# Attention of a hybrid trunk: probabilities turned in 32x32 blocks on VectorE, and every engine in a written order

## The chip, the cores and the metric

The kernel runs on one core of one Trainium2 chip. The metric is the device time of one launch in microseconds (us), the lower the better. A comparison of two kernels takes several runs of each on the same chip. Times of single instructions and waits come from one profiled execution of a kernel.

The engines are named as the profile names them: PE is TensorE (matmuls), PEld its weight loads, DVE is VectorE, ACT is ScalarE, POOL is GpSimd, and SP is the engine from whose queue most loads are issued. Each has its own instruction stream and runs it in order; semaphores connect them. Data lies in SBUF, with 128 partitions, and in PSUM, into which PE writes, here in banks of 512 fp32 columns.

## What is computed

Two layers over 512 latent tokens and 128 context tokens of width 1024. Layer 0 is grouped-query attention with 16 query heads over 4 key/value heads of 64 dimensions; layer 1 is a gated linear recurrence. Both have an adaLN modulation and a post-LayerNorm. The change is in layer 0. The part of the reference that it touches:

```python
def _block_attention(q, k, v):
    ...
    def one_block(q_blk):
        s = jnp.einsum('bqkgd,bskd->bkgqs', q_blk.astype(jnp.float32), kf) * scale
        p = jax.nn.softmax(s, axis=-1)
        return jnp.einsum('bkgqs,bskd->bqkgd', p, vf).astype(q.dtype)

def _attn_latent(h, ctx_k, ctx_v, w_in, q_gain, k_gain, w_out):
    q, k, v, g = _attn_project(h, w_in, q_gain, k_gain)
    ...
    keys = jnp.concatenate([ctx_k.astype(k.dtype), k], axis=1)
    vals = jnp.concatenate([ctx_v.astype(v.dtype), v], axis=1)
    o = _block_attention(q, keys, vals)
    return _attn_out(o, g, w_out)
```

`_attn_project` has the RMS norm of queries and keys, the lines left out the rotary positions, and `_attn_out` multiplies by silu(g) and by `w_out`. Latent queries read 640 keys, 128 cached and 512 latent; context queries read the 128 context keys. All is fp32. Projections and scores split an operand into a high and a low part (type fp32r) and add the products; the product of probabilities and values is a plain fp32 matmul, which stands as two matmul instructions in the trace.

## The kernel before

The program has a lead-in (modulation, key/value projection, first query projection, gate projections), a woven attention, the output projection with the norm, and the recurrent layer. The change is in the woven attention, which goes over the 4 key/value heads `c`, each with 4 query heads `h`.

*A front* (`front`, L812) is one query head and 128 latent queries: four matmuls, two halves of 320 keys by a high and a low key part (`score_mms`, L722), into one of two double banks. DVE takes the negated maximum (L817), ACT the exponential with its sum (L820). Two calls later (`defer`, L733, and `tick`, L739), DVE takes the reciprocal and POOL scales the probabilities `p` (L824, L825). There are 64 fronts and four of the prompt (`prompt_unit`, L767).

*The turn* (`trans`, L828): the product with the values needs keys on partitions, so PE transposes `p` into PSUM, in ten 128x128 pieces per unit of two fronts (L832), and ACT or DVE copies them to SBUF (`keep_pt`, L726).

*The product* (`apply`, L841): for two heads and 256 queries, five key blocks of 128; the values are the stationary operand (128 keys by 64 columns, `vv`, L499), and the two heads lie in the two halves of the array's columns (`av_mms`, L747). DVE multiplies the result into the gate `gs` in place (L755).

Between these run side jobs: the query projections of heads 1 to 3 (`q_gen`, L591: 15 token tiles of 24 matmuls, norm and rotary positions on DVE, a split and transposes), 16 chunks of the modulation (`ada_gen`, L308, whose weights stream in from DRAM), the split of the gated result (`split_gs`, L941) and two pieces of the output weights. `att_gen` (L851) and `weave` (L85) make the source order: 0.7 steps of the side jobs after each step of attention. The engines don't follow that order strictly: a scheduler of the tile layer places each engine's instructions by priority and estimated readiness, so that one that is ready can go ahead of one that waits. SP's loads go through a queue of their own in the order of `order` (L366), two pieces ahead (`pump`, L196).

Of the kernel before, what the change touches and what calls it, by code (L numbers as in the profile page):

```python
# [11 lines left out]
F32 = mybir.dt.float32  # L12
# [21 lines left out]
ADA_CUT = (4, 8, 12)  # L34
# [6 lines left out]
D_SCALE = 2  # L41
D_OUTS = 2
SIDE_T = 2.2
SIDE_B = 0.7
# [87 lines left out]
def hybrid_step(ctx: ExitStack, tc: tile.TileContext, a: dict, o: dict):  # L132
# [141 lines left out]
    def ada_row(ps):  # L274
        row = rowp.tile([P, CW], F32, tag="row", name="row")
        nc.vector.tensor_copy(row, ps[:, :CW])
        return row
# [30 lines left out]
    def ada_gen(chunks):  # L308
        todo, last = None, None
        for l, c in chunks:  # L310
            ps = bank1("adaps")
            ada_mms(ps, l, c, 0)
            if last:
                last()
            last = todo and ada_out(*todo)
            yield
            ada_mms(ps, l, c, 1)
            yield
            todo = (l, c, ada_row(ps))
        if last:  # L320
            last()
        if todo:
            last = ada_out(*todo)
            yield
            if last:
                last()
                yield

# [30 lines left out]
    ADA_AT = (0,) + ADA_CUT + (len(ADA),)  # L359
    ADA_B = [ADA[ADA_AT[n]:ADA_AT[n + 1]] for n in range(4)]  # L360

# [6 lines left out]
    for c in range(3):  # L368
        order.extend(pieces("attn_w_in", c + 1))
        order.extend(ada_pieces(ADA_B[c]))  # L370
    order.extend(ada_pieces(ADA_B[3]))
    order.extend(("attn_w_out", nh, i) for nh, i in PIECES)
# [53 lines left out]
    with pool("xin", 1) as xin:  # L426
        rope = xin.tile([P, 2, TS, HD], F32, name="rope")
        ck = prep.tile([P, CW], F32, tag="ck", name="ck")
# [44 lines left out]
        for ft in range(KT):  # L473
# [4 lines left out]
            row = ada_row(ps)  # L478
# [20 lines left out]
    vv = kvp.tile([P, 6, CW], F32, name="vv")  # L499
# [18 lines left out]
    def rms_apply(ps, n, rstd, off=0):  # L518
        w = n * CW
        qn = prep.tile([P, 2 * CW], F32, tag="qn", name="qn")  # L520
# [5 lines left out]
    def rope_apply(qn, tt0, n, cos, sin, g, r=None):  # L526
# [3 lines left out]
        if tt0 == TS:  # L530
# [3 lines left out]
        u = prep.tile([P, 2 * CW], F32, tag="u", name="u")  # L534
        nc.vector.tensor_tensor(heads4(u[:, :w], n), heads4(qn[:, :w], n),
                                view(sin, tt0 * HD, [[HD, n], [0, 4], [1, HD]]), ALU.mult)
        nc.vector.tensor_tensor(heads4(r[:, :w], n), heads4(qn[:, :w], n),
                                view(cos, tt0 * HD, [[HD, n], [0, 4], [1, HD]]), ALU.mult)
# [29 lines left out]
    def q_split(r, tt0, n, odd, X, alloc):  # L568
# [4 lines left out]
        nc.vector.tensor_tensor(view(s2, HD * (1 - odd), [[P, 4 * n], [1, HD]]), rv, hv.bitcast(F32), ALU.subtract)  # L573
# [11 lines left out]
    def tok_unit(w, tt0, n, name):  # L585
        ps = bank1(name)
        for i in range(n):
            yield from tok_gen(ps[:, i * CW:(i + 1) * CW], w, tt0 + i, hhi, hlo)
        return ps

    def q_gen(c, X):  # L591
        w = Weights("attn_w_in", c, (nc.vector, nc.vector))
        yield
        yield
        pend = None
        for tt0, n in UNITS:
            ps = yield from tok_unit(w, tt0, n, "qmm")
            rstd = rms_stat(ps, n)
            yield
            if pend:  # L600
                for i in range(pend[1]):
                    pend[0](i)
                    yield
            else:
                yield
            yield
            qn = rms_apply(ps, n, rstd)
            r = rope_apply(qn, tt0, n, cosq, sinq, qg)
            yield
            pend = (q_split(r, tt0, n, c % 2, X, bank1), n)  # L610
        yield
        for i in range(pend[1]):
            pend[0](i)
            yield
# [124 lines left out]
    def tick():  # L739
# [4 lines left out]
        for _, fn in due:  # L744
            fn()
# [757 lines left out]
```

## Time and profile before

| | |
|---|---|
| median of three runs | 892.8 us (889.97 to 896.09) |
| the profiled execution | 891.1 us, of which the span of instructions is 889.3 |
| busy share of the span | PE 95%, DVE 61%, ACT 42%, POOL 24% |
| woven attention | 138.8 to 368.0 us |
| lead-in before it, from the gate projections on | 75.0 to 138.8 us |
| output projection, norm and recurrent layer after it | 368.0 to 889 us |

A row of a group reads: line, engine, operation, output<-inputs, shape, count | busy us, mean ns of one | idle time of the engine just before them and what ended it. Tile shapes of matmuls such as 128\*64 are rows by columns of the array. A row of waits reads: who waited <- for what: us in total, times, longest. Matmuls are pipelined, so that their durations overlap; the distance of two starts is what one costs in a stream.

### The profile page before, as it was taken

Reading aid. Unit: us, or ns where it says so; the run is one execution under the profiler, and the core shown is the slowest. Engines: PE = TensorE matmul, PEld = TensorE weight load, DVE = VectorE, ACT = ScalarE, POOL = GpSimd, SP = SyncE. Lnnn points to the kernel's source line nnn. Section 1 sums busy time; section 2 is a strip of 40 time slices with the busy share of each in tenths; the row PEclk is TensorE's granted clock in tenths of the full one; section 3 lists DMA queues with packets and bytes.
Section 4 is the critical chain, followed back from the end, with each engine's and each line's share of the span. In section 5 each row is a group of like instructions: output and inputs, shape, how many; then the busy total and the mean of one; then the engine's idle time right before and its main releaser. Section 6 shows DMA issues by size and latency. Waiting matters only on the chain.

```text
span 889.3 us, 19146 instructions
## 1 busy us (share of the span) xinstructions
PE 844.8 (95%) x8076; PEld 736.4 (83%) x8076; DVE 539.0 (61%) x960; ACT 371.2 (42%) x732; POOL 212.6 (24%) x247
## 2 busy tenths in 40 slices
PE   6898999989999899999999999999999999988995
PEld 3588999858858656778899999999999999986774
DVE  3466335646655644676446677576768585758495
ACT  2232437545554745522244454444444444443200
POOL 0032003323323724510000133233333224110110
PEclk9999999999999999999999999999999999998998
DMA  9831210042051066271131313232332313232121
GB/s 359 328 107 54 81 39 25 2 164 75 1 194 45 3 218 208 90 242 48 57 117 51 102 56 117 63 98 77 91 95 79 101 55 107 64 111 99 54 95 71
DMA packets 30182, 89.84 MB, mean 101 GB/s; under 512 B 4401, under 2 KB 9009, under 8 KB 29073
## 3 DMA queue, kind: packets, MB, share of 16 engines
q1 hardware_dynamic: 19728, 72.03, 24.1%
q0 software_dynamic: 3168, 9.31, 3.7%
q10 hardware_dynamic: 7200, 7.29, 2.6%
q8 instruction: 63, 1.03, 0.5%
q14 instruction: 23, 0.18, 0.1%
HBM read 79.44 MB, written 9.18 MB: 100 GB/s over the span
## 4 chain that ended last, share of the span: by engine, by line
PE 76%; DMA 8%; DVE 7%; POOL 3%; ACT 3%; issue 2%; ACTq 0%; DVEq 0%; POOLq 0%
PE rps L1106 7%; PE rps L1107 6%; PE rps L1108 6%; PE vgps L1096 5%; PE pot L750 4%; PE vgps L1098 4%; PE vgps L1097 4%; PE pt L832 4%; DMA raw<-in_ada_w 3%; PE outp L984 3%; PE outp L985 3%; PE outp L986 3%; PE lv L1236 2%; PE adaps L262 2%; PE sc L723 2%
## 5 line engine op out<-in xcount | busy, mean ns | idle before, releaser
L1106 PE MATMUL rps<-h1hi,rhi 128*128 128x320 f32 x368 | 118.2, 321 | 0.0
L1107 PE MATMUL rps<-h1lo,rhi 128*128 128x320 f32 x368 | 113.7, 309 | 0.0
L1108 PE MATMUL rps<-h1hi,rlo 128*128 128x320 f32 x368 | 113.3, 308 | 0.0
L825 POOL TENSOR_SCALAR p<-p,rc 128x640 f32<-128x640 f32 x64 | 52.1, 816 | 104.1 <-DVE rc L824 101.2
L1106 PEld LDWEIGHTS rps<-h1hi,rhi 128*128 128x128 f32 x368 | 69.1, 188 | 1.3
L1107 PEld LDWEIGHTS rps<-h1lo,rhi 128*128 128x128 f32 x368 | 69.3, 188 | 0.0
L1108 PEld LDWEIGHTS rps<-h1hi,rlo 128*128 128x128 f32 x368 | 69.1, 188 | 0.0
L820 ACT ACTIVATE p<-sc,nm 128x640 f32<-128x640 f32 x64 | 51.1, 798 | 41.3 <-DVE nm L817 33.4
L817 DVE TENSOR_REDUCE nm<-sc 128x1 f32<-128x640 f32 x64 | 52.4, 820 | 24.3 <-PE sc L724 23.6
L222 DVE TENSOR_TENSOR rlo<-raw,rhi 128x1024 fp32r<-128x1024 f32 x32 | 46.1, 1441 | 33.9 <-ACT rhi L221 33.9
L1264 POOL COPY At<-near 32x160 f32<-32x160 f32 x32 | 14.0, 437 | 196.6 <-DVE near L1226 195.6
L1214 ACT COPY kc<-A 128x640 f32<-128x640 f32 x40 | 32.2, 805 | 59.0 <-DVE A L1245 51.6
L221 ACT CAST rhi<-raw 128x1024 fp32r<-128x1024 f32 x32 | 33.6, 1049 | 51.6 <-PE rps L1107 47.4
L832 PE MATMUL pt<-ident,p 128*128 128x128 f32 x320 | 51.2, 279 | 1.4 <-DVE pts L728 0.8
L1096 PE MATMUL vgps<-rhi,h1hi 128*128 128x256 f32 x180 | 51.4, 286 | 1.2 <-ACT h1hi L938 1.2
L1098 PE MATMUL vgps<-rhi,h1lo 128*128 128x256 f32 x180 | 50.5, 280 | 0.4 <-DVE h1lo L939 0.4
L1097 PE MATMUL vgps<-rlo,h1hi 128*128 128x256 f32 x180 | 50.5, 280 | 0.0
L750 PE MATMUL pot<-pts,vv 128*64 128x256 f32 x320 | 50.0, 390 | 0.0
L832 PEld LDWEIGHTS pt<-ident,p 128*128 128x128 f32 x320 | 36.8, 142 | 12.9 <-issue 6.7
L728 ACT COPY pts<-pt 128x512 f32<-128x512 f32 x64 | 36.0, 588 | 23.5 <-PE pt L832 23.2
L723 PE MATMUL sc<-kk,X 128*128 128x320 f32 x128 | 43.2, 345 | 0.4 <-ACT p L820 0.4
L332 PE MATMUL gps<-hhi,whi 128*128 128x320 f32 x128 | 40.8, 319 | 2.4 <-ACT X L582 2.4
(257 smaller groups left out, 2399.2 us busy)
## 6 DMA issues: line engine op xcount, KB each, us to landing
raw<-in_rec_w_in SPq DMA_DIRECT2D x40, 512.0 KB, 3.8
raw<-in_ada_w SPq DMA_DIRECT2D x32, 512.0 KB, 4.4
raw<-in_ada_w SPq DMA_DIRECT2D x8, 1024.0 KB, 11.3
raw<-in_attn_w_in SPq DMA_DIRECT2D x16, 512.0 KB, 4.2
raw<-in_attn_w_out SPq DMA_DIRECT2D x8, 512.0 KB, 4.4
raw<-in_rec_w_out SPq DMA_DIRECT2D x8, 512.0 KB, 4.1
h<-in_xT SPq DMA_DIRECT2D x8, 320.0 KB, 10.8
x1d<-y SPq DMA_DIRECT2D x5, 512.0 KB, 2.6
```

Of the source, the lines that this page charges most:

```text
L723: nc.tensor.matmul(out, X[:, h, t0:t0 + P], kk[:, c, k0:k1], start=True, stop=False)
L750: nc.tensor.matmul(pot[j * HD:(j + 1) * HD, :CW], vv[:, slot, c * HD:(c + 1) * HD], moving[j], start=first, stop=last)
L817: nc.vector.tensor_reduce(nm[:, 0:1], sc[:, :, :320], AX.XY, ALU.max, negate=True)
L820: nc.scalar.activation(halves(p[:]), sc[:, :, :320], AF.Exp, bias=nm[:, 0:1], accum_out=su[:, 0:1])
L825: nc.gpsimd.tensor_scalar(p, p, rs[:, 0:1], 1.0, ALU.mult, ALU.mult)
L832: nc.tensor.transpose(pt[:, i * 256 + q * P:i * 256 + (q + 1) * P], ps[q][:, (k0 + i) * P:(k0 + i + 1) * P], ident)
L1096: nc.tensor.matmul(out, h1hi[:, k, t], hi, start=(k == 0), stop=False)
L1097: nc.tensor.matmul(out, h1hi[:, k, t], lo, start=False, stop=False)
L1098: nc.tensor.matmul(out, h1lo[:, k, t], hi, start=False, stop=(k == KT - 1))
L1106: nc.tensor.matmul(ps[:, j, :320], hi[:, k, :], h1hi[:, k, t], start=(k == 0), stop=False)
L1107: nc.tensor.matmul(ps[:, j, :320], hi[:, k, :], h1lo[:, k, t], start=False, stop=False)
L1108: nc.tensor.matmul(ps[:, j, :320], lo[:, k, :], h1hi[:, k, t], start=False, stop=(k == KT - 1))
```

## The change

*The turn goes to DVE.* A DVE transpose (`nc.vector.transpose`) turns each 32x32 block of `p` where it lies: element (query 32i+q, key 32j+k) goes to partition 32i+k, column 32j+q of the tile `T`. So keys lie on partitions in blocks of 32, and the four partition groups i belong to four groups of queries. The 320 PE transposes and their copies out of PSUM are gone.

*The product is cut to fit.* A matmul takes 32 partitions: 32 keys by 64 value columns stationary, and 32 keys by 128 queries (32 of each of the four query blocks) moving. Partition group i needs the values of all keys on its own 32 partitions, so the values are written once to DRAM (`vd`) and fetched four times into `vrep`, four DMAs per key/value head from POOL's queue, with two heads in SBUF at a time. A block (`sample_out`) serves two heads and all 512 queries: 20 key blocks, two heads `e` (column halves), four partition groups `i`, 160 matmuls in a row, each group `i` into a PSUM bank of its own. There are eight blocks; the prompt's product is 32 smaller matmuls behind every second one. The gating is four operations of 128 columns per block and four of 64 per prompt.

*The order is written out.* For each head `c` there are 17 steps: 16 fronts and the prompt's at step 8. At step n come the front, the scaling of front n-1, the turn of front n-2; blocks stand at steps 2 and 10. `make_plan` puts the side jobs at numbered steps (`ADA_AT`, `WQ_AT`, `WO_AT` and the numbers in it). Within `tc.manual_schedule` PE, DVE, ACT and POOL keep exactly that order.

*Smaller moves.* Modulation rows go from DVE to ACT; ACT copies query tiles out of PSUM; two of three rotary products and the query's low part go from DVE to POOL, and half of the weights' low parts too. The ring of probability tiles has 4 in place of 7. POOL's DMA scratch is 4096 bytes.

PE, around one product. Before, in the attention of one of the later key/value heads: `pt` are the turned pieces, `sc` scores, `qps` turned queries, `pot` products, `qmm` query projections.

```order
L580 MATMUL qps<-identr,qs_3067 128x128 x4
L832 MATMUL pt<-ident,p 128x128 x2
L723 MATMUL sc<-kk,X_2141 128x320
L724 MATMUL sc<-klo,X_2141 128x320
L723 MATMUL sc<-kk,X_2141 128x320
L724 MATMUL sc<-klo,X_2141 128x320
L580 MATMUL qps<-identr,qs_3067 128x128 x4
L832 MATMUL pt<-ident,p 128x128 x4
L750 MATMUL pot<-pts,vv 64x256
L832 MATMUL pt<-ident,p 128x128 x4
L750 MATMUL pot<-pts,vv 64x256 x9
L339 MATMUL qmm<-whi,hhi 128x256
```

After, at step 10 of the second head: `T` is the turned tile and `vrep` the repeated values.

```order
L741 MATMUL sc<-kk,X_1682 128x320
L742 MATMUL sc<-klo,X_1682 128x320
L843 MATMUL pot<-T,vrep 64x128 x160
L741 MATMUL sc<-kk,X_1682 128x320
L742 MATMUL sc<-klo,X_1682 128x320
L741 MATMUL sc<-kk,X_1682 128x320
L742 MATMUL sc<-klo,X_1682 128x320
L281 MATMUL adaps_2876<-small,row 128x2 x2
```

The turned pieces are gone from PE, and a product stands as one row of 160 between two fronts.

DVE, in the attention before: `nm` is the maximum, `rc` the reciprocal, `pts` a turned piece, `qn`, `r` and `qs` queries, `row` and `shsc` modulation, `gs` the gate.

```order
L817 TENSOR_REDUCE nm<-sc 128x1
L824 RECIPROCAL rc<-su 128x1
L522 TENSOR_TENSOR qn<-qmm,rstd 128x256
L531 TENSOR_TENSOR r<-qn,gains 128x256
L824 RECIPROCAL rc<-su 128x1
L573 TENSOR_TENSOR qs_2660<-r,qs_2660 128x4x64
L276 COPY row<-adaps 128x256
L293 TENSOR_TENSOR shsc_84<-adaps_2719,small 128x4
L776 TENSOR_REDUCE nmp<-pscp 128x4
L755 TENSOR_TENSOR gs<-pot,gs 128x256
L728 COPY pts<-pt 128x256
```

After, at steps 10 and 11 of the second head:

```order
L817 TENSOR_REDUCE nm<-sc 128x1
L824 RECIPROCAL rc<-su 128x1
L792 STREAM_TRANSPOSE Tp<-pp 128x512
L617 TENSOR_TENSOR qn<-qn,rstd 128x512
L849 TENSOR_TENSOR gs<-pot,gs 128x4x32 x4
L817 TENSOR_REDUCE nm<-sc 128x1
L824 RECIPROCAL rc<-su 128x1
L830 STREAM_TRANSPOSE T<-p 128x640
L610 TENSOR_REDUCE ss<-sq 128x4
L186 TENSOR_SCALAR rs_t<-ss 128x4
L529 TENSOR_TENSOR r<-r,u 128x512
```

Each step now has maximum, reciprocal and a transpose, and the gating stands between the maximum of the block's step and that of the next.

POOL, at steps 2 to 5 of the second head, after:

```order
L825 TENSOR_SCALAR p<-p,rc 128x640
L488 DMA vrep<-vd 32x24x64 x4
L825 TENSOR_SCALAR p<-p,rc 128x640
L525 TENSOR_TENSOR u<-qn,sinq 128x512
L527 TENSOR_TENSOR r<-qn,cosq 128x512
L825 TENSOR_SCALAR p<-p,rc 128x640
```

The value fetches and the rotary products stand between the scalings, which before had the powers of the norms and the splits for neighbours.

The diff, cut to what the text speaks of:

```diff
-    ADA_AT = (0,) + ADA_CUT + (len(ADA),)
+    ADA_AT = ((6, 11, 14), (0, 5, 8, 13), (0, 5, 8, 13), (0, 4, 7, 11, 14))
+    WQ_AT = (10, 11)
+    WO_AT = (5, 6)
...
+    vd = dram.tile([NKV, TT + 1, P, HD], F32, name="vd")
+    def load_values(c):
+        vrep[c] = kvp.tile([P, 24, HD], F32, tag="vrep", name="vrep", bufs=2)
+        for i in range(4):
+            nc.gpsimd.dma_start(vrep[c][32 * i:32 * i + 32], vd[c].rearrange("s (j p) d -> p (s j) d", j=4))
...
+    def sample_front(c, h, a, T):
+        sc = bank2("sc")
+        for n, (k0, k1) in enumerate(HALVES):
+            score_mms(sc[:, n, :320], Xs[c], c, h, a * P, k0, k1)
...
         def trans():
-            pt = bank1("ptp")
-            for h in range(4):
-                s = (h % 2 * 2 + h // 2) * P
-                nc.tensor.transpose(pt[:, s:s + P], st["p"][:, h * P:(h + 1) * P], ident)
-            st["s"] = keep_pt(pt, 512, nc.scalar.copy)
...
+            nc.vector.transpose(T[h % 2][:, a, :], p)
+        defer(2, scale)
+        defer(3, trans)
+
+    def sample_out(c, pr, T, prompt):
+        with tc.high_priority():
+            pots = [pop[0].tile([P, 512], F32, tag="po", name="pot")] + [bank1("pot") for _ in range(3)]
+            for j in range(20):
+                for e in range(2):
+                    for i in range(4):
+                        r = slice(32 * i, 32 * i + 32)
+                        out = pots[i][e * HD:(e + 1) * HD, :P].rearrange("p (a q) -> p a q", a=TS)
+                        nc.tensor.matmul(out, vrep[c][r, j, :], T[e][r, :, 32 * j:32 * j + 32],
+                                         start=(j == 0), stop=(j == 19))
+            if prompt:
+                prompt[0](pots)
+        for i in range(4):
+            gt = view(gs, (2 * c + pr) * NT + 32 * i, [[P, TS], [1, 32]])
+            nc.vector.tensor_tensor(gt, pots[i][:, :P].rearrange("p (a q) -> p a q", a=TS), gt, ALU.mult)
...
+    AV_AT = (2, 10)
+    def make_plan():
+        plan = [([], [], []) for _ in range(17 * NKV + 8)]
...
+            for d, fn in enumerate((q.square, q.stat, q.norm, q.rope)):
+                for u, at in first.items():
+                    put(at + d, 1, fn, u)
...
+    def att_gen():
+        for n in range(17 * NKV):
+            c, s = divmod(n, 17)
...
+            if s == 8:
+                prompt = prompt_unit(c)
+                prompt[0]()
+            else:
+                m = s - (s > 8)
+                sample_front(c, m // 4, m % 4, T[m // 8])
             tick()
...
+            if s in AV_AT:
+                if s == AV_AT[1]:
+                    sample_out(c, 0, T[0], None)
+                elif c:
+                    sample_out(c - 1, 1, last[0], last[1])
+                    if c < 3:
+                        load_values(c + 1)
...
-    weave(att, side, SIDE_B)
-    side.finish()
+    E = mybir.EngineType
+    with tc.manual_schedule(engines={E.PE, E.DVE, E.Activation, E.Pool}):
+        drain(att)
```

More of the change, by code (lines that the diff above doesn't have):

```diff
@@ L367, in hybrid_step @@
         order.extend(pieces("attn_w_in", c))
[L368 to L372, printed above, removed]
+    order.extend(pieces("attn_w_in", 1))
+    todo = list(ADA)
+    for c in range(NKV):
+        for s in range(17):
+            if c < 2 and s in WQ_AT:
+                order.append(("attn_w_in", c + 2, WQ_AT.index(s)))
+            if c == 3 and s in WO_AT:
+                order.append(("attn_w_out",) + PIECES[WO_AT.index(s)])
+            if s in ADA_AT[c]:
+                order.extend(ada_pieces([todo.pop(0)]))
+    order.extend(("attn_w_out", nh, i) for nh, i in PIECES[2:])
     order.extend(("rec_w_in", h, i) for h in range(RH) for i in range(5))
@@ L477, in hybrid_step @@
                 kv_split(ft // 2)
[L478 removed]
+            row = ada_row(ps, nc.vector.tensor_copy)
             if ft:
@@ L901, in hybrid_step, with trans, apply @@
-    side = Side()
-    att = att_gen(side)
+            defer(2, scale)
+            def trans():
+                st["T"] = sm.tile([P, 512], F32, tag="Tp", name="Tp", bufs=1)
+                nc.vector.transpose(st["T"][:, :512], p[:, :512])
+            defer(3, trans)
+        def apply(pots):
+            T = st["T"]
+            for j in range(4):
+                for e in range(2):
+                    for i in range(4):
+                        r = slice(32 * i, 32 * i + 32)
+                        t = T[r, :512].rearrange("p (a e j q) -> p e j a q", a=2, e=2, j=4)[:, e, j]
+                        out = pots[i][e * HD:(e + 1) * HD, P:P + HD].rearrange("p (a q) -> p a q", a=2)
+                        nc.tensor.matmul(out, vrep[c][r, 20 + j, :], t, start=(j == 0), stop=(j == 3))
@@ new lines, in ada_item, with mms, row, out @@
+    def ada_item(l, c, at, plan):
+        cell = {}
+        def mms():
+            cell["ps"] = bank1("adaps")
+            for i in range(2):
+                ada_mms(cell["ps"], l, c, i)
+        def row():
+            cell["row"] = ada_row(cell["ps"])
+        def out():
+            cell["last"] = ada_out(l, c, cell["row"])
+        n = at + 3 if (at + 2) % 17 in AV_AT else at + 2
+        plan[at][2].append(mms)
+        plan[at + 1][0].append(row)
+        plan[n][2].append(out)
+        if l == 0:
+            plan[n + 1][2].append(lambda: cell["last"]())
```

365 lines of the change are left out of this document (168 added, 197 removed).

## The prediction

> **What bounds the kernel now.** I read the page first, then the busy time by stretches, then the groups, waits and timeline inside the one stretch that the change touches.
>
> ```profile
> span 889.3 us, 19146 instructions
> PE 844.8 (95%) x8076; PEld 736.4 (83%) x8076; DVE 539.0 (61%) x960; ACT 371.2 (42%) x732; POOL 212.6 (24%) x247
> ```
>
> ```profile
> 75.00:138.80 63.80, 61.08 (x428) 60.44 (x427) 22.14 (x37) 24.84 (x48) 4.05 (x2) 0.97 0.17 57
> 138.80:368.00 229.20, 219.76 (x1727) 166.63 (x1725) 132.37 (x295) 125.13 (x272) 81.93 (x85) 1.00 0.27 91
> 368.00:889.00 521.00, 500.67 (x5504) 461.37 (x5504) 344.81 (x551) 200.20 (x382) 113.85 (x147) 0.99 0.30 91
> ```
>
> The columns of the stretches are its length, then the busy time of PE, PEld, DVE, ACT and POOL, and the granted clock. TensorE is busy 95% everywhere. The woven attention runs from 138.8 (last gate projection) to 368.0 (first output projection), 229.2 us, of which PE is busy 219.8, DVE 132.4, ACT 125.1 and POOL 81.9. PE is the bound there, and the next engine has 97 us to spare. The clock is 1.00, so there is nothing to win from it. The stretches before and after keep their compute instructions. The five stores of values on ACT's queue and the first eight fetches of value copies on POOL's come before it; two of the fetches stand ahead of the power for the queries' norm, and the gate projections, with PE busy for 61 of 63.8 us, cover them. So the sum is made on the one stretch.
>
> ```profile
> L832 PE MATMUL pt<-ident,p 128*128 128x128 f32 x320 | 51.2, 279 | 1.4 <-DVE pts L728 0.8 <-POOL p L825 0.5
> L750 PE MATMUL pot<-pts,vv 128*64 128x256 f32 x320 | 50.0, 390 | 0.0
> ...
> L750 PEld LDWEIGHTS pot<-pts,vv 128*64 128x64 f32 x320 | 23.5, 136 | 14.1 <-issue 6.3 <-DVE pts L728 0.2
> ```
>
> ```profile
> PEld pt L832 <- issue: 6.7, 17, 0.4
> PEld pot L750 <- issue: 6.3, 31, 0.4
> ```
>
> ```profile
> 206.85 1.03 PE L832 MATMUL pt<-ident,p 128*128 128x128 f32 x8
> 207.64 0.36 PE L339 MATMUL qmm<-whi,hhi 128*128 128x256 f32 x1
> ...
> 365.00 2.46 PE L750 MATMUL pot<-pts,vv 128*64 128x256 f32 x20
> ...
> 475.76 0.62 PE L1236 MATMUL lv<-A,kc 128*32 128x32 f32 x40
> 476.32 0.39 PE L1096 MATMUL vgps<-wspare,h1hi 128*128 128x256 f32 x1
> ```
>
> The first two of these rows are the work that the change replaces: 320 transposes and 320 value matmuls (160 in the source; each fp32 matmul runs as two passes). Durations there overlap, so I take starts. Eight transposes hold PE from 206.85 to 207.64, 0.099 us each. Twenty value matmuls, one whole product, take 2.46 us: ten pairs at 0.246 us, the two halves of a pair (columns 0-63 and 64-127 of the array) side by side. The two "issue" rows are PE standing still, for 0.2 us on average at the value matmuls (6.3 by 31), where it goes from one kind of tile to another.
>
> **PE: what goes and what comes.** Gone: 336 transposes (16 of them the prompt's) by 0.099, 33.3 us; 16 products by 2.46, 39.4; four prompt products of two pairs, 2.0; the issue waits, 13.0. Together 88 us. Added: eight blocks of 160 value matmuls. Each works on 32 rows by 64 columns of the array with 128 moving columns, and eight of them (four row groups, two column halves) cover the array. If all eight run side by side, a block is 20 key blocks of two passes, 40 passes of half a pair's 256 columns, 0.123 us each: 4.9 us, eight times 39.4. This is the same arithmetic as before on the same array. Four prompt blocks of eight passes at 64 columns add 2.0, and 16 changes of tile shape at 0.2 add 3.2. Together 45, so PE's busy time goes from 220 to about 177.
>
> Whether four row groups run side by side no row shows: every matmul of the trace has 128 rows. The nearest rows are the column groups: 40 matmuls of 32 columns, in four groups, hold PE from 475.76 to 476.32, 14 ns each with its own weight load, so 320 of them can be issued in 4.5 us, less than the 4.9 that they stream. The other end is one row group at a time, four times 4.9. I take side by side, since the column groups are the nearest case, each row group reads its own partitions, and each writes a PSUM tile of its own. [...]
>
> **DVE: what goes and what comes.**
>
> ```profile
> L817 DVE TENSOR_REDUCE nm<-sc 128x1 f32<-128x640 f32 x64 | 52.4, 820 | 24.3 <-PE sc L724 23.6
> L728 DVE COPY pts<-pt 128x256 f32<-128x256 f32 x32 | 13.4, 419 | 7.1 <-PE pt L832 6.7
> L824 DVE RECIPROCAL rc<-su 128x1 f32<-128x1 f32 x64 | 10.1, 158 | 17.0 <-ACT p L820 15.5 <-POOL p L825 1.0
> L276 DVE COPY row<-adaps 128x256 f32<-128x256 f32 x16 | 6.8, 422 | 16.7 <-PE adaps L262 16.7
> L755 DVE TENSOR_TENSOR gs<-pot,gs 128x256 f32<-128x256 f32 x16 | 6.7, 416 | 2.0 <-PE pot L750 2.0
> L222 DVE TENSOR_TENSOR wlo<-raw,whi 128x1024 fp32r<-128x1024 f32 x5 | 6.1, 1219 | 0.7 <-ACT whi L221 0.7
> L573 DVE TENSOR_TENSOR qs<-r,qs 128x512 fp32r<-128x512 f32 x6 | 5.4, 894 | 1.4 <-ACT qs L572 1.4
> L535 DVE TENSOR_TENSOR u<-qn,sinq 128x512 f32<-128x512 f32 x6 | 5.0, 836 | 0.2
> L537 DVE TENSOR_TENSOR r<-qn,cosq 128x512 f32<-128x512 f32 x6 | 4.1, 679 | 0.0
> L573 DVE TENSOR_TENSOR qs<-r,qs 128x256 fp32r<-128x256 f32 x3 | 2.1, 692 | 1.2 <-ACT qs L572 1.2
> L755 DVE TENSOR_TENSOR gs<-potp,gs 128x256 f32<-128x256 f32 x4 | 1.6, 412 | 0.0
> L293 DVE TENSOR_TENSOR shsc<-adaps,small 128x4 f32<-128x4 f32 x8 | 1.3, 162 | 9.4 <-PE adaps L285 9.4
> ```
>
> ```profile
> L1245 DVE TENSOR_TENSOR A<-A,T 128x640 f32<-128x640 f32 x32 | 26.3, 822 | 8.9 <-issue 4.7 <-PE lv L1236 2.7 <-PE lv L1242 0.9
> L1136 DVE TENSOR_SCALAR T<-s,omlb,lbt 128x640 f32<-128x640 f32 x16 | 11.4, 714 | 0.0
> L1313 DVE TENSOR_TENSOR on<-on,g 128x640 f32<-128x640 f32 x8 | 9.6, 1195 | 0.3
> ```
>
> Of the stretch's 132.4 us DVE loses the copies of turned probabilities (13.4), the modulation rows (6.8, to ACT), two of the three rotary operations (5.0 and 4.1, to POOL), the query low parts (5.4 and 2.1, to POOL) and two weight low halves (2.4). The gating grows from 20 to 48 smaller operations: 4 columns cost 0.162 and 256 cost 0.416, so about 0.29 for 128 and 0.22 for 64, 12.8 us in place of 8.3. That leaves 97.7. Then 64 block transposes of 128x640 come in. No transpose on DVE is in the trace; DVE's operations of that size, from SBUF to SBUF, take 0.714 to 1.195 us. I take the row that is commonest, 0.822: 52.6, and 2.6 for four prompt tiles. DVE: 153 us.
>
> DVE can't fill all of the stretch. Its order is now the source's, and while a block of 160 matmuls holds PE (4.9 and two changes at 0.2) no new scores come; DVE has one step's work left (0.82 + 0.16 + 0.82 = 1.8) and then stands before the gating, with the next maximum queued behind. That is 3.5 us eight times, 28. The rotary sum stays on DVE behind two products on POOL.
>
> ```profile
> L820 ACT ACTIVATE p<-sc,nm 128x640 f32<-128x640 f32 x64 | 51.1, 798 | 41.3 <-DVE nm L817 33.4 <-DVE rc L824 4.8 <-DVE mx L919 1.0
> L728 ACT COPY pts<-pt 128x512 f32<-128x512 f32 x64 | 36.0, 588 | 23.5 <-PE pt L832 23.2
> L825 POOL TENSOR_SCALAR p<-p,rc 128x640 f32<-128x640 f32 x64 | 52.1, 816 | 104.1 <-DVE rc L824 101.2 <-DMA raw<-in_attn_w_out 2.3 <-PE pot L750 0.5
> L939 POOL TENSOR_TENSOR hlo<-gs,hhi 128x640 fp32r<-128x640 f32 x7 | 11.2, 1619 | 2.4 <-PE qmm L341 2.4
> L191 POOL TENSOR_TENSOR rstd<-rs_t,mhalf 128x8 f32<-128x8 f32 x6 | 9.9, 1644 | 8.3 <-DVE rs_t L190 8.3
> L786 POOL TENSOR_TENSOR pp<-pp,rcp 128x512 f32<-128x512 f32 x4 | 4.2, 1039 | 84.1 <-DVE rcp L785 84.1
> ```
>
> ```profile
> L1341 POOL DMA_DIRECT2D rx<-x1d x20 | 11.0, 549 | 11.3 <-DMA x1a<-rx 11.2
> ...
> PE adaps L262 <- DMA raw<-in_ada_w: 0.6, 2, 0.3
> ```
>
> From the reciprocal on, POOL does one scaling (0.82) and two products of 128x512 (1.04 each), 2.9 us, of which DVE fills its transpose and one small operation, some 1.4. So 1.5 us is lost, six times: 9. Altogether DVE's stretch is 153 + 28 + 9 = 190 us, longer than PE's 177, and it sets the pace.
>
> The other engines stay below that. POOL goes from 82 to about 116: twelve products 12.5, nine query low parts some 10 and three weight halves some 8 (by the row of 1619 for 640 columns), eight DMA issues at 0.55. The four DMAs that fetch a value copy wait for the last block that reads the old one; queued behind them on POOL is one scaling, and behind that a transpose, late by at most 1.2 us, twice: inside the rounding. ACT loses 36 and gains 16 copies of rows and 15 of queries. SP's loads are issued in the new order of use; PE lost only 0.6 us to them and each chunk still has two ahead, so nothing. A value copy, fetched four times from DRAM, is needed 25 steps after it is issued, some 70 us at 190 us for 66 steps; the two fronts issued before the stretch stay there.
>
> The sum: 229.2 becomes 190, a gain of 39. The profiled execution took 891.1 us in all, so its like would take 852; the median of the three runs is 1.7 above it, so I forecast 854. With transposes at 0.714 DVE's stretch would be 183, and with the blocks hidden entirely it would be PE's 177: 852 less 7 to 13. The forecast's own range is 838 to 866.
>
> **The rivals.** First, two row groups at a time. A block takes 9.8 us, eight times 4.9 more: 893, no change. Here lies the point of decision, since 39 by eight is 4.9. For it: no row shows row groups. Against: the column groups do run together.
>
> Second, the other side, one row group at a time: 14.7 more per block, 118 in all, 972, slower. It would show at the value matmuls and nowhere else. [...]
>
> Third, the fixed order costs more than I count, or transposes are dear. At 1.195 they add 24 us: 878. The same is lost where POOL's forty longer operations (nine powers, twelve rotary products, nine query parts, four weight halves, six splits) each hold one scaling, and so a transpose, for 0.6 us. For it: POOL's share rises, and PE, DVE, ACT and POOL can no longer slip past one another. Against: in the trace of before a scaling waits 101 us for DVE in all and delays PE by little.
>
> **How the numbers follow.** Forecast 0.57; fixed order or dear transposes, around 878, 0.21; two row groups at a time, 893, 0.11; one at a time or loads in turn, 972 or more, 0.11. A change below 1% (8.9 us) can't be told from none here. Faster takes the first and nearly all of the second, 0.76; same takes most of the third, 0.12; slower 0.12. The range from 838 to 890 holds the first two cases and a part of the third, about 0.8.
>
> **What would show it.** The 160 matmuls of a block span 4.9 us, with eight starting within a few tens of ns; 20 would be one row group at a time. The block transposes take about 0.82 us. In the stretch DVE is busy some 153 us of 190 and its idle time lies before the gating, released by the value matmuls, and before the rotary sum, released by POOL; PE now waits at the scores for ACT. If PE still has no idle time there and the stretch is over 215 us, the value matmuls are mis-sized; if DVE's busy time is over 175, the transposes are; if both are as counted and the stretch is over 205, the fixed order is the cause.

## The result and the profile after

The changed kernel takes 928.6 us (median of four runs, 927.03 to 929.99) against 894.4 before on the same chip (four runs, the three of 892.8 and one more): 1.038 times the time, 95% interval 1.031 to 1.044. The forecast was 854, and slower had a chance of 0.12.

The page of the changed kernel has a span 35.9 us longer, with less of PE's work in it:

```profile
span 925.2 us, 23413 instructions
PE 819.6 (89%) x10220; PEld 735.3 (79%) x10220; DVE 552.4 (60%) x984; ACT 345.8 (37%) x695; POOL 257.8 (28%) x287
...
q8 instruction: 80, 1.31, 0.6%
```

PE's busy share went from 95 to 89%. The last row is the queue that brings in PE's instructions: packets, MB, share. (PE's 20440 matmuls and weight loads over 80 packets, and 16152 over 63 in the kernel before, are some 256 instructions a packet.) The lead-in ends at 141.4 instead of 138.8 us, the first output projection starts at 404.7 instead of 368.0, and what follows keeps its 520 us. So nearly all of the loss is in the woven attention: 263.3 us where before had 229.2 and the forecast 190. The stretches of after, the whole attention first, then 20 us in the middle of it (length, busy time of PE, PEld, DVE, ACT, POOL, granted clock, DMA share, GB/s):

```profile
141.40:404.70 263.30, 193.04 (x3875) 163.87 (x3873) 144.74 (x320) 101.30 (x242) 120.31 (x116) 0.88 0.27 88
250.00:255.00 5.00, 3.53 (x28) 3.27 (x26) 2.62 (x8) 1.82 (x3) 3.06 (x4) 1.00 0.01 3
255.00:260.00 5.00, 0.00 (x0) 0.00 (x0) 3.76 (x7) 1.03 (x3) 2.01 (x2) 0.84 0.15 39
260.00:265.00 5.00, 3.24 (x18) 3.24 (x19) 2.16 (x5) 2.34 (x5) 2.32 (x2) 0.50 0.18 66
265.00:270.00 5.00, 4.36 (x40) 3.38 (x38) 2.25 (x4) 1.93 (x5) 1.24 (x2) 0.97 0.48 168
```

No engine fills the stretch any more: PE stands for 70 us of it, DVE for 119. And PE is slower when it works. The granted clock is 0.88 on average; the four small rows show one place: PE stands from 253.5 to 261.8, and then works at 0.50 before it is back at 0.97. At the gap from 323.7 to 331.1 it is the same, with 0.50 up to 336. Over the stretch, busy time times what the clock lacks adds up to 21.5 us, so that at full clock PE's work would be some 172, by estimate. That standing always lowers the clock, or that being busy raises it, isn't shown: in a later run, the first without the order, PE was busy for 5 us and stayed at 0.50.

What PE waited for in the stretch, and the groups of DVE and PE that waited most (busy us, mean ns | idle before, releaser):

```profile
PE qps L570 <- POOL qs L563: 23.0, 7, 8.2
PE pot L843 <- issue: 12.3, 9, 2.1
PE sc L741 <- ACT p L820: 5.4, 8, 1.6
PE adaps L258 <- DMA raw<-in_ada_w: 4.7, 2, 4.0
```

```profile
L843 PE MATMUL pot<-T,vrep 32*64 32x128 f32 x2560 | 48.5, 289 | 19.9 <-issue 12.3 <-DVE T L830 4.5 <-DVE gcol L292 1.3
...
L830 DVE STREAM_TRANSPOSE T<-p 128x640 f32<-128x640 f32 x64 | 52.8, 825 | 2.6 <-POOL p L825 2.5
L817 DVE TENSOR_REDUCE nm<-sc 128x1 f32<-128x640 f32 x63 | 51.1, 813 | 35.6 <-PE sc L742 35.6
L849 DVE TENSOR_TENSOR gs<-pot,gs 128x128 f32<-128x128 f32 x32 | 7.2, 284 | 45.0 <-PE pot L803 26.9 <-PE pot L843 18.1
L529 DVE TENSOR_TENSOR r<-r,u 128x512 f32<-128x512 f32 x6 | 4.2, 692 | 20.2 <-POOL r L527 20.2
```

Of DVE's 119 us of standing, 45.0 lie before the gating, 35.6 before the maximum, for scores, and 20.2 before the rotary sum. The transposes cost what they should. On PE two things stand out: its wait before the turned queries (23.0), and the blocks, where PE waits for "issue" (the profile shows nothing that it waited for). The timeline of the third block, PE's value matmuls only:

```profile
239.49 0.45 PE L843 MATMUL pot<-T,vrep 32*64 32x128 f32 x8
240.71 2.54 PE L843 MATMUL pot<-T,vrep 32*64 32x128 f32 x161 [0.78 <-DVE T L830]
245.31 2.08 PE L843 MATMUL pot<-T,vrep 32*64 32x128 f32 x128 [2.06 <-issue]
249.04 0.66 PE L843 MATMUL pot<-T,vrep 32*64 32x128 f32 x23 [1.65 <-issue]
```

128 matmuls run in 2.08 us, so the row groups do run side by side, but the block lasts 10.2 us, because PE stands still in it three times: once for DVE's last transpose (0.78 us), twice for "issue" (2.06 and 1.65). From first start to last end the eight blocks take 68.4 us, 8.5 each; without their holes the median is 5.7.

The longest wait for queries is a chain over four engines (before that, the power of the norm on POOL ends at 253.7):

```profile
254.95 1.26 POOL L527 TENSOR_TENSOR r<-qn,cosq 128x512 f32<-128x512 f32 x1
256.24 0.69 DVE L529 TENSOR_TENSOR r<-r,u 128x512 f32<-128x512 f32 x1 [3.58 <-POOL r L527]
258.06 0.82 DVE L817 TENSOR_REDUCE nm<-sc 128x1 f32<-128x640 f32 x1
259.75 0.61 ACT L562 CAST qs<-r 128x512 fp32r<-128x512 f32 x1
260.44 1.27 POOL L563 TENSOR_TENSOR qs<-r,qs 128x512 fp32r<-128x512 f32 x1 [0.53 <-ACT qs L562]
261.76 1.01 PE L570 MATMUL qps<-identr,qs 128*128 128x128 f32 x6 [8.23 <-POOL qs L563]
```

The maximum at 258.06 belongs to scores that PE had finished at 253.5. DVE reaches it late, since it waited 3.6 us for POOL's product and then split a weight piece for 1.2; ACT's cast stands behind that step's exponential; and PE, two fronts ahead, may not pass the transposes.

### The profile page after: what moved, and what is told of

Same layout as the page of the kernel before. It is cut to its first block, busy times and chain, and to the rows that moved or that the text cites. A ratio compares the mean times of both kernels' runs of the same rounds, so it can differ in the third digit from the quotient of the medians.

```text
span 925.2 us, 23413 instructions
## 1 busy us (share of the span) xinstructions
PE 819.6 (89%) x10220; PEld 735.3 (79%) x10220; DVE 552.4 (60%) x984; ACT 345.8 (37%) x695; POOL 257.8 (28%) x287
## 4 chain that ended last, share of the span: by engine, by line
PE 71%; DVE 11%; POOL 6%; issue 5%; ACT 4%; DMA 2%; DVEq 0%; SPq 0%; ACTq 0%; POOLq 0%
PE rps L1161 6%; PE rps L1162 6%; PE rps L1163 6%; PE pot L843 5%; PE vgps L1151 4%; PE vgps L1153 4%; PE vgps L1152 4%; PE outp L1038 3%; PE outp L1039 3%; PE outp L1040 3%; PE adaps L258 2%; PE lv L1291 2%; PE gps L307 2%; PE gps L309 2%; PE gps L308 2%
## 5 line engine op out<-in xcount | busy, mean ns | idle before, releaser
L843 PE MATMUL pot<-T,vrep 32*64 32x128 f32 x2560 | 48.5, 289 | 19.9 <-issue 12.3
L843 PEld LDWEIGHTS pot<-T,vrep 32*64 32x64 f32 x2560 | 42.0, 139 | 26.0 <-issue 16.0
L830 DVE STREAM_TRANSPOSE T<-p 128x640 f32<-128x640 f32 x64 | 52.8, 825 | 2.6 <-POOL p L825 2.5
L258 PE MATMUL adaps<-raw,sil 128*32 128x256 f32 x384 | 32.0, 450 | 12.9 <-ACT sil L170 6.2
```

What stands on the lines that cost most here:

```text
L830: nc.vector.transpose(T[h % 2][:, a, :], p)
L843: nc.tensor.matmul(out, vrep[c][r, j, :], T[e][r, :, 32 * j:32 * j + 32], start=(j == 0), stop=(j == 19))
```

## The experiments

All times are medians beside runs of the kernel before on the same chip, with the ratio to it and its 95% interval. The five kernels that leave a part of the product out ran once each and have no interval; the others ran two to ten times. Three theories were set against each other: A, the query chain in the fixed order; B, the blocks; C, the fixed order as such.

**Order, chain and block, one at a time.** The order taken away:

```diff
-    with tc.manual_schedule(engines={E.PE, E.DVE, E.Activation, E.Pool}):
-        drain(att)
+    drain(att)
```

> The changed kernel without the fixed order: the scheduler places each engine's instructions again; the transposes on DVE, the 32x64 products and the moves of query work stay. The changed kernel took 928.6 us. Theory A, the fixed order holds PE behind the query chain (PE stood 23.0 us before the turned queries, waiting for POOL, and its clock fell to 0.50 behind such gaps): those waits go, 23 us and most of the some 20 us lost to the clock, about 885 to 895. Theory B, the blocks are mis-sized (8.5 us each, with holes named issue, instead of 4.9): the blocks cost the same in any order, at most 10 us are won, 918 to 929.

916.6 us, ratio to before 1.026 (1.023 to 1.029). The wait for queries is gone, but the blocks fell apart: the scheduler put the matmuls of one row group together.

```profile
184.25 7.26 PE L843 MATMUL pot<-T,vrep 32*64 32x128 f32 x66
```

```profile
185.00:190.00 5.00, 5.00 (x50) 5.00 (x48) 0.00 (x0) 0.00 (x0) 0.00 (x0) 0.50 0.00 0
```

Here 66 matmuls take 7.26 us, pairs 0.213 us apart at a clock of 0.50. So this run changed two things at once and decides nothing on the order (it is mended below). The second row stands out too: PE is busy throughout and the clock stays at 0.50.

The query work back on DVE, with a step's split ahead of its other query jobs:

```diff
-            self.st[u] = rope_apply(self.qn[u], tt0, n, cosq, sinq, qg, None, nc.gpsimd)
+            self.st[u] = rope_apply(self.qn[u], tt0, n, cosq, sinq, qg, None, nc.vector)
...
-            self.back[u] = q_split(self.st[u], tt0, n, self.c % 2, Xs[self.c], bank1, nc.gpsimd)
+            self.back[u] = q_split(self.st[u], tt0, n, self.c % 2, Xs[self.c], bank1, nc.vector)
...
```

> The two rotary products and the low part of the query go back from POOL to DVE (and a step's split stands ahead of its other query work, so that DVE doesn't wait for itself); all else is the changed kernel, fixed order too. Theory A, the query chain through POOL holds PE: DVE's 20.2 us before the rotary sum and PE's 23.0 us before the turned queries go for the most part, DVE works 17 us more; 895 to 908. Theory B, the blocks: the time stays within 6 us of 928.6.

915.8 us (1.025, 1.022 to 1.029). DVE's wait before the rotary sum is gone; PE's before the queries is halved:

```profile
PE qps L570 <- DVE qs L563: 10.8, 5, 4.4
```

The turned queries two steps later:

```diff
-                put(at + 5, 2, q.turn, u)
+                put(at + 7, 2, q.turn, u)
```

> The turned queries stand two steps later in the order (PE transposes at step at+7 instead of at+5); no work changes. Theory A, PE waits because the turn stands too early for the chain DVE, POOL, ACT, POOL: PE's 23.0 us before the turned queries fall below 5 and the clock behind them stays up; 893 to 908. Theory B, the blocks, or a chain that is only late as a whole: PE waits as long at the next score, within 6 us of 928.6.

916.9 us (1.026, 1.018 to 1.035). PE's waits for queries are gone, yet only 12 of 23 us came back: its wait at the scores for ACT grew from 5.4 to 9.9 us, and that for loads from 4.7 to 7.7. Both runs speak for A at half its price.

Half of the columns in each value matmul, which leaves out half of the product:

```diff
...
-                        nc.tensor.matmul(out, vrep[c][r, j, :], T[e][r, :, 32 * j:32 * j + 32],
+                        nc.tensor.matmul(out, vrep[c][r, j, :], T[e][r, :2, 32 * j:32 * j + 32],
...
```

> Leaves out half of the product: each value matmul moves 64 columns in place of 128 (queries of the first two blocks only; the gating uses them twice). The number of instructions is the same, the streaming is halved. Theory B1, a block is bound by the streaming of its columns: a block's 5.7 us without holes fall to about 3, 20 us are won, 908. Theory B2, a block is bound by its 640 instructions (16 KB fetches of the instruction queue come 3.4 us apart inside a block, some 17 us apart elsewhere): the holes grow by what the streaming loses, a block stays at 7 us or more, the time at 920 or more.

928.9 us: nothing won. Then half the key blocks instead, which halves the number of instructions too:

```diff
-            for j in range(20):
+            for j in range(10):
...
-                                         start=(j == 0), stop=(j == 19))
+                                         start=(j == 0), stop=(j == 9))
```

> Leaves out half of the product: only key blocks 0 to 9 of 20, so a block is 80 value matmuls (320 instructions in place of 640) of the full 128 columns; the streaming is halved as in the run with half the columns. If a block is bound by its instructions, it falls from 8.5 us to 3 to 4.5 us, eight times some 4.5, and the DVE wait behind it with it: 885 to 900. If the price lies at a block's start and end (the wait for the last turned tile, the change of tile shape), only the 2.8 us of streaming per block go, as they should have with half the columns: 905 or more.

902.7 us, 26 less. The value matmuls in the changed kernel, with half the columns, and with half the key blocks (ns least/median/most, first and last start; below it, idle time before all value products for want of instructions: us, times):

```profile
L843 PE MATMUL pot<-T,vrep x2560: 264/268/472, 171.7 to 400.7; 32*64 32x128 f32 x197
...
  issue: 16.9, 12
```

```profile
L843 PE MATMUL pot<-T,vrep x2560: 211/263/366, 172.6 to 402.5; 32*64 32x64 f32 x197
...
  issue: 26.1, 14
```

```profile
L843 PE MATMUL pot<-T,vrep x1280: 267/268/472, 171.8 to 377.3; 32*64 32x128 f32 x183
...
  issue: 2.4, 2
```

With half the streaming the holes grow by 9 us and the eight blocks still take 62.7 us; with half the streaming and half the instructions the holes are nearly gone and they take 35.0. So a block is bound by its instructions; the run with four heads, below, halves these alone and agrees. They come in packets of 16 KB on the instruction queue: in the third block of the changed kernel at 242.9 and 246.4 and the next at 251.9, in the attention of the kernel before 14 to 20 us apart, and after each hole that the packets explain PE goes on 1.3 to 1.6 us after one has landed. Between the two holes of the third block lie 128 matmuls with their loads, 256 instructions, one packet. A block has 640 instructions, two loads and two matmuls per product, so two and a half such packets, and PE stands until they have landed (2.06 and 1.65 us in the third block).

**Both cures, the clock, and cut blocks.** Both query edits together:

> The rotary products and the query's low part back on DVE and the turned queries two steps later, together. Alone they gave 915.8 and 916.9, some 12 us each. Theory A1, both cure the same wait (PE before the turned queries, 23.0 us): together little more than one alone, 910 to 915. Theory A2, one cures DVE's wait before the rotary sum and the other PE's: they add up, 901 to 908.

908.7 us (1.016, 1.009 to 1.022), 20 less than the changed kernel, between the two expectations: they cure in part the same wait.

Useless matmuls at three of the places where PE stood longest, behind which its clock was at 0.50 for 3.5 to 5.9 us after it went on. If the standing there is what lowers the clock, it should now stay up, and the time fall if the clock sets it:

```diff
...
+            for _ in range(fill):
+                nc.tensor.matmul(pt[:, :320], kk[:, 0, :P], kk[:, 0, :320], start=True, stop=True)
             for h in range(4):
                 s = i * 512 + h * P
                 nc.tensor.transpose(pr[:, h * P:(h + 1) * P], s2[:, s:s + P], identr)
...
```

> The changed kernel with useless matmuls of 128x320 (44, 18 and 40 of them, some 0.145 us each, 14.8 us in all) in front of the turned queries at the three places where PE stood 8.2, 3.8 and 7.4 us; they are overwritten. [...]

928.1 us (924.3 to 928.8): no change. The three filled places, the changed kernel first:

```profile
255.00:275.00 20.00, 12.25 (x100) 10.43 (x100) 10.90 (x21) 7.64 (x17) 7.22 (x8) 0.83 0.23 80
290.00:310.00 20.00, 16.08 (x129) 13.70 (x128) 8.77 (x18) 7.75 (x23) 8.52 (x9) 0.83 0.29 75
325.00:345.00 20.00, 11.99 (x80) 8.22 (x80) 12.04 (x26) 8.43 (x19) 8.69 (x10) 0.66 0.23 81
```

```profile
255.00:275.00 20.00, 17.16 (x136) 14.96 (x134) 10.58 (x21) 7.29 (x17) 7.14 (x9) 0.91 0.27 79
290.00:310.00 20.00, 18.81 (x166) 16.71 (x165) 9.41 (x19) 8.66 (x27) 9.07 (x10) 1.00 0.36 94
325.00:345.00 20.00, 16.07 (x99) 12.61 (x97) 11.79 (x24) 8.40 (x19) 8.08 (x9) 0.74 0.26 81
```

The clock rises from 0.83 to 0.91 and 1.00 at the first two, but only from 0.66 to 0.74 at the third. DVE does about the same work in the same time at the first and third, 7% more at the second. So at two of these places the clock was up where PE no longer stood, and raising it there gained nothing that can be told from noise. What the low clock costs in all isn't shown: in the stretch it still lasts 48 us, against 61 in the changed kernel.

Both cures, and each block cut in two with a front between:

```diff
...
-            for j in range(20):
+            for j in range(10 * part, 10 * part + 10):
...
```

> As the run with both cures, and each block is cut into two halves of ten key blocks, the first at the end of step 2 or 10, the second behind the next front; nothing is left out. If the holes in a block are fetches of instructions that come too late, other work between the halves covers a part of them: the issue waits at the value matmuls fall from 12 to 14 us to some 5, and DVE gets its scores earlier, 8 to 15 us below the run with both cures. If the price of a block is its matmuls whatever stands between, no gain, within 3 us of it.

907.3 us (1.014, 1.007 to 1.021), the same as without the cut. The issue waits at the value matmuls fell from 11.7 to 6.9 us, but with a front in it a block ends no earlier: the eight take 68.9 us from first start to last end, against 67.1. Why the time didn't come back wasn't tested.

**The order again.** Free order, but a block's matmuls kept in program order; then the query cures on top:

```diff
...
+                        tc.keep_in_program_order(
                             nc.tensor.matmul(out, vrep[c][r, j, :], T[e][r, :, 32 * j:32 * j + 32],
...
```

> As the run without the fixed order, but the 160 matmuls of a block are kept in program order, so that the four row groups stay interleaved. In the run without the order (916.6) the scheduler had put the matmuls of one row group together, and pairs of them started 0.107 us apart at full clock, one row group at a time. If the order itself costs (theory C), this kernel is 885 to 900. If only the blocks cost and the order little, it stays at 905 to 915.

> The same on top of both query cures (rotary products and low part on DVE, the turned queries later): free order, blocks kept. Theory A, the query chain only hurts because PE may not pass it: with a free order the cures bring nothing more, within 4 us of the run without them. If POOL's longer operations hurt in any order (each holds a scaling), 6 to 12 us below it.

900.8 us (1.008, 1.005 to 1.012) and 904.8 us (1.012, 1.008 to 1.017). Taking the fixed order away gives back 28 us, and without it the query cures bring nothing. PE's wait before the turned queries, 23.0 us in the fixed order, is gone there without them, so the chain hurt PE mainly because nothing could pass it. In the free order PE waits most for something else:

```profile
PE sc L741 <- ACT p L820: 14.4, 10, 6.0
PE pot L844 <- issue: 8.1, 7, 1.6
```

**Fewer instructions with nothing left out.** Two heads share their values, so one matmul can move both heads' columns:

```diff
...
-                        out = pots[i][e * HD:(e + 1) * HD, :P].rearrange("p (a q) -> p a q", a=TS)
-                        nc.tensor.matmul(out, vrep[c][r, j, :], T[e][r, :, 32 * j:32 * j + 32],
+                        out = pots[i][e * HD:(e + 1) * HD, :2 * P].rearrange("p (n a q) -> p n a q", n=2, a=TS)
+                        nc.tensor.matmul(out, vrep[c][r, j, :], T[e][r, :, :, 32 * j:32 * j + 32],
...
```

> The changed kernel, fixed order and all, with four blocks in place of eight: a block serves the four heads of a key/value head, each value matmul moving 256 columns (two heads that share the values) in place of 128. Half the instructions, the same streaming, nothing left out. To make room the turned tiles are held once (two tiles of two heads), so that DVE's next turn waits for the block, and values and probability tiles have one buffer less. If instructions bound the blocks, a block is some 10 to 11 us with few issue holes, four of them 42 in place of 68, and with half the prompt's changes of shape the time is 898 to 908. If streaming bound them, four blocks take 60 or more and the time is 920 or more; the single buffers can take back some 5 us of either.

> The same four blocks without the fixed order, the matmuls of a block kept in program order (the run with eight blocks in this form took 900.8). If the two causes are the instructions of the blocks and the fixed order, their gains add up: 870 to 882, faster than the kernel before. If the single buffers of the turned tiles make DVE and PE take turns, little is won over 900.8: 893 to 905.

926.6 us (1.037, 1.034 to 1.040) and 905.4 us (1.013, 1.010 to 1.016). The blocks did as expected: four of them, 45.3 us instead of 68.4, and no issue wait to speak of. Without holes a block takes 9.4 to 10.0 us in three of the four, some 4.8 per two heads. The time didn't follow:

```profile
L842 PE MATMUL pot<-T,vrep x1280: 373/375/630, 209.2 to 401.8; 32*64 32x256 f32 x183
...
  issue: 0.3, 1
...
  DVE T L829: 23.2, 3
```

The last row is who waited for the blocks: DVE, 23.2 us before its next turn, since the turned tiles had to be held once. I had put that at 5 us. PE's waits grew too, at the scores for ACT from 5.4 to 12.1 us and for loads from 4.7 to 10.8, and none of the three was taken away on its own. Here a cheaper block, which DVE had to wait out, was worth no more than a dear one.

**Do the causes add up, and what is the rest?** Half the key blocks in the free order, then one key block of 20, in the fixed and in the free order (the rest of the product is left out):

> Leaves out half of the product (key blocks 10 to 19), without the fixed order and with the matmuls of a block kept in order. The order alone was worth 27.8 us (928.6 to 900.8), half the blocks alone 26.0 (to 902.7). If the two causes add up: 872 to 880. If they are two names of one wait (DVE without scores while PE is in a block): 888 to 900.

> Leaves out nearly all of the product: one key block of 20, so a block is 8 matmuls; fixed order and everything else as in the changed kernel. It prices the blocks and, by what is left, the rest. If the rest costs what the prediction counted (DVE's 153 us of work, 9 of waits for POOL, no blocks to stand before), the stretch is some 165 to 175 us and the time 828 to 840. If the rest is mis-sized too (the query chain in the fixed order, loads that come late, the low clock behind waits): 860 to 885.

> Leaves out nearly all of the product, one key block of 20, without the fixed order. If the fixed order is what holds the rest up, 825 to 845. If the rest waits for something else, for instance for loads or for the chain score, maximum, exponential, scaling, turn itself, it stays within 12 us of the run with one key block and the fixed order.

893.2, 892.8 and 867.0 us. The order (28) and half the blocks (26) together bring 35, not 54: the two share much of their waits. And the kernel with nearly no value product at all takes 892.8 us in the fixed order, as long as the kernel before with its product. Its stretch, and its largest wait; then the stretch in the free order:

```profile
141.40:370.40 229.00, 164.58 (x1444) 134.66 (x1442) 145.79 (x320) 101.40 (x242) 121.31 (x117) 0.79 0.32 100
```

```profile
PE qps L570 <- POOL qs L563: 22.1, 9, 6.8
```

```profile
141.40:345.40 204.00, 158.37 (x1445) 129.65 (x1443) 146.51 (x320) 101.18 (x241) 118.38 (x116) 0.85 0.36 109
```

The forecast's count has 165 to 175 us for this. In the fixed order it is 229, though DVE does 146 us of work and PE 165 at a clock of 0.79.

**Steps of uneven work.** Cutting the trace at each step's first score matmul (PE) and maximum (DVE), up to the first output projection, gives each step's work. In the changed kernel the 68 steps sum to 197 us on PE (the last gate projections and the slow clock in it) and 146 on DVE; if each step lasts as long as its busier engine, the sum is 222. With both cures it is 195, 159 and 226, for a stretch of 245. (The 202, 162 and 232 of the expectation come out if the last step is taken some 7 us into the output projection.) So two modulation chunks were moved from the first head's steps to the last two heads', where PE has least to do, and the others were spread anew:

```diff
-    ADA_AT = ((6, 11, 14), (0, 5, 8, 13), (0, 5, 8, 13), (0, 4, 7, 11, 14))
+    ADA_AT = ((14,), (4, 8, 11, 14), (0, 6, 9, 11, 14), (0, 4, 7, 9, 11, 14))
```

> On top of both query cures with the fixed order (908.7): two of the modulation's chunks move from the first head's steps, where PE has up to 6 us of work in a step and DVE 1.6, to the last two heads' steps, where DVE's 1.6 us set the pace and PE has 1 to 2. No work changes. By the busy times of that run's steps, PE 201.7 and DVE 162.3 in sum, but 231.9 us if each step lasts as long as the busier of the two, for a stretch of 245. If a fixed order pays step by step (sum of maxima), evening out wins 3 to 6 us, 903 to 906. If only the sums count, nothing, 907 to 910.

> The same move of two chunks in the kernel with free order and blocks kept (900.8). The scheduler evens out by itself, so less is to be won: 898 to 902. If it wins as much as with the fixed order, 895 to 898, and then PE's work per step counts there too.

898.3 us (1.005, 1.003 to 1.008) in the fixed order, 10 less for the same work, and 902.3 (1.010, 1.005 to 1.015) in the free one, no change. The stretch with both cures, before and after the move:

```profile
141.40:386.20 244.80, 191.97 (x3882) 163.74 (x3880) 157.71 (x341) 101.21 (x242) 97.52 (x96) 0.90 0.30 94
```

```profile
141.40:377.20 235.80, 188.51 (x3877) 162.71 (x3876) 157.28 (x341) 100.69 (x242) 97.32 (x96) 0.91 0.31 98
```

DVE's work is the same, PE's 3 us less, the stretch 9 us shorter. That the place of the side jobs counts in a fixed order is shown. That it counts by the sum of maxima isn't: that sum fell only from 226 to 223, so most of the gain must lie in waits inside steps. Which ones, no run here shows.

The last run has both cures, the even steps, the cut blocks and the first projections a step later:

> On top of both query cures and the evened side jobs (898.2): each block in two halves with a front between, as in the earlier run where that won 1.4 us, and the first head's query projections one step later, so that PE's 2.8 us before the split of their weights fall under other work. If blocks hold DVE up by standing in one piece and the start costs its waits, 890 to 895, at or below the kernel before. If PE's issue waits and its low clock set the time whatever the order, 896 to 899.

895.9 us, 1.002 times the kernel before (0.999 to 1.004), between the two expectations, so it doesn't decide between them. The 33 us are back with DVE's transposes and the cut product in place, by the order and by the rotary products and low parts that went back to DVE. No version with its whole product is faster than the kernel before.

## Why the prediction was wrong, by its own steps

- **PE's work.** 177 us forecast, some 172 at full clock: right. One term had a weak source: the 13.0 us of "issue" are waits of the weight loads (PEld), while PE's own rows of the same two groups show 1.4 and 0.0 us of idle time. The transposes (0.822 forecast, 0.825 measured), DVE's sum (153; 144.7) and POOL's (116; 120.3) were close too, though POOL's rotary products took 1.27 to 1.30 us in place of 1.04; the row of 1619 ns for 640 columns, which priced the low parts, would have given that. Work was not the error.
- **Row groups side by side.** Right, so neither rival on them (two at a time, one at a time) came true. The four-head blocks show 4.8 us per two heads for the streaming that was put at 4.9. One row group alone (the run without order) has pairs 0.213 us apart at half the clock, so an estimated 17 us per block at the full clock against 5.7 without holes: 3.0 times. But these blocks are held by the issue of their instructions; by the 4.8 us of the four-head blocks it is an estimated 3.5. Loads in turn, which the chances name beside one row group at a time, no run shows; the blocks took 8.5 us, 5.7 without holes.
- **A block of 4.9 us and two changes at 0.2.** Mis-sized: 8.5. The price was taken from the columns it streams, with the instructions only bounded (320 issued in 4.5 us). With half the columns the median block without holes is still 4.7 us, so some 15 ns per matmul, near the 14 of the prediction, was the right rate of issue; what the prediction left out is whether instructions arrive at that rate. Half the blocks' instructions and streaming are worth 26 us alone, 8 in the free order.
- **"The clock is 1.00, so there is nothing to win from it."** It left out what there was to lose: in the changed kernel the clock falls to 0.50 at gaps such as those of 8.2 and 7.4 us, and the change was going to give PE such gaps. An estimated 21.5 us of PE's time went to the low clock, though filling three of the gaps gained nothing.
- **The sum.** This is the step that failed. It took DVE's 153 us of work, added 28 and 9 of waits, and called 190 the stretch. The waits it named were there, at 45.0 and 20.2 us in place of 28 and 9, but beside them DVE stood 36 us for scores, a wait that the sum put at nothing, while PE was itself held by the query chain, the loads and the blocks. These three are 101 of the 119 us that DVE stood, where the sum has 37. "Six times 1.5" for the rotary sum counted POOL's two products and not the power ahead of them nor the step behind them, where the exponential, cast and low part stand between DVE's sum and PE. The kernel with nearly no product prices this: 892.8 us in the fixed order where the count has 828 to 840.
- **The third rival, the fixed order**, had 0.21 and 878. It was the right mechanism with too small a price, and with PE left out of it: it was seen as POOL's long operations holding scalings, and what it did was hold PE before the turned queries. The free order gives back 28 us.
- **"If both are as counted and the stretch is over 205, the fixed order is the cause."** By this test the answer would have been the order alone. The free order stands at 900.8, so the test was too simple: it had no case for two causes that share their waits.
- **Small ones.** The lead-in was put at nothing and costs 2.7 us. The loads were put at nothing, and PE waits 4.7 us for two of them, in some of the experiments 10. No engine waited for the value copies.

What stays open: in the free order, with nearly no product, PE still stands 46 us of 204. Its largest waits there are at the scores for ACT (11.8), for loads (6.6) and for queries (6.1); none of these was taken away on its own. Nor does any run show how much of the fixed order's price goes through PE's low clock.

## What to carry to other kernels

Work taken from the busiest engine counts only as far as the others can run ahead: in a fixed order with two buffers between engines, add up what each step waits for, with the whole chain of a side job in it, rather than the engines' totals (here DVE's total and two of its waits gave 190 us for a stretch of 263). A matmul cut into small tiles has to be priced by its instructions as well as by its columns (here 8.5 us a block, where the columns gave 4.9); look for "issue" waits and for packets on the instruction queue. And where a change will make TensorE stand, ask what its clock does afterwards (here 0.50 from within a gap of 8.2 us until 3.5 us after it).

## What the hardware showed that was not expected

- A row of 640 PE instructions without other work runs into its own instruction fetch: 16 KB packets 3.4 to 3.5 us apart inside a block, holes of 1.0 to 2.1 us between them (up to 3.8 with half the columns), where in the attention of the kernel before they were 14 to 20 us apart and PE had no such wait at its product (0.0 us idle).
- Four row groups by two column halves start a matmul every 13 to 15 ns, each with its own weight load (the median of most blocks of the changed kernel).
- PE busy all of 5 us with one row group and two column halves stayed at a clock of 0.50 (185 to 190 us of the first run without order). Being busy in the records was not enough to raise the clock there; why wasn't tested.
